# A third and a second seven-product group in the down stages of both FFNs

## The chip, the cores and the metric

The kernel runs on one core of one Trainium2 chip. The metric is the device time of one execution in microseconds (us), the median of several runs. The engines are TensorE (PE in the profile, with PEld for its weight loads), VectorE (DVE), ScalarE (ACT), GpSimd (POOL) and SyncE (SP), whose queue issues nearly all DMAs.

## What is computed

One encoder layer on 256 rows of width 2048, all in float32, with large feed-forward parts:

```python
def swiglu(h, w_gate, w_up, w_down):
    return (jax.nn.silu(h @ w_gate) * (h @ w_up)) @ w_down

x = x + 0.5 * swiglu(rms_norm(x, ffn1_norm), ffn1_w_gate, ffn1_w_up, ffn1_w_down)
...   # input projection, SSM, stick-breaking attention, output projection
x = x + 0.5 * swiglu(rms_norm(x, ffn2_norm), ffn2_w_gate, ffn2_w_up, ffn2_w_down)
...   # per-layer embedding
```

D_FF is 5632. The change is in the product with `w_down`: (256 x 5632) by (5632 x 2048), once in each FFN.

## The kernel before, in words

**Products in three parts.** Every float32 matrix is split into a high part (a cast to fp32r on ScalarE, L181) and a low part (the difference, on VectorE, L184). A product is then high x high, low x high and high x low, three matmuls of 128x512 each. Weights come from DRAM as tiles `raw` of 1 MB (512 rows by 512 columns, 128x2048 floats on chip); a split handles half of one (`whi`, `wlo`, 128x1024).

**The down stage** (from L649, in `ffn`) makes the four output blocks of 512 columns in two pairs, `n = 0` and `n = 2`. The inner dimension has 11 groups of 512 rows, `kb` 0 to 10. A plan (L673 to L676), one for each pair, says in which order the groups come and how each is computed:

- `cK` is a column step (`Seven.column`, L524): group K, first for one output block, then for the other. Each block takes two weight halves, and each half 12 matmuls (two row tiles of the output), so a column step has 48 matmuls, four weight splits and one split of the activations (`act`, L652: `hhi`, `hlo`).
- `sK` is a seven-product group (`Seven.chunk`, L490): group K for both blocks at once, by a Strassen-like scheme with 7 products instead of 8. Each product has 6 matmuls, 42 in all. It takes both weight tiles at once and forms four sums of weight halves on VectorE (`add`, L485 to L488, tile `sum`), which are split like weights (`shi`, `slo`); three other products split weight halves as they are (`whi`, `wlo`). It also takes sums of the activations, `sum_forms` (L432): four additions of 128x256 (L441, tile `rows`) and a split (`nhi`, `nlo`), beside the split of the activations themselves.
- `a5` is the rest, groups 5 to 10, first all of them for one block, then all for the other. There the activations are split again for the second block.

**Banks.** Products 2 and 4 (one block) and 3 and 8 (the other) end in the banks that the column steps use too. Products 1, 5, 6 and 7 have banks of their own; when the last `s` step of a pair has been issued, `opened` (L660 to L671) is put off to the next step: one copy on ScalarE (L663), and on VectorE two additions (L664, L669) and six of L658 that add these banks to the residual `x`. `end` (L686) adds the other banks to `x` and starts the norm of the next stage (`Normed.block`, L370): transposes on VectorE (L216), 32 small DMAs through SP's queue (L229), and later the split by L191 on ScalarE and L193 on VectorE, four of each for a block. For the two blocks of the first pair this falls into the second pair.

**What sets the order.** Each engine executes its instructions in the order of the program. A planner fixes that order when the kernel is built, from the order of the Python code, the readiness that it foresees and the free buffers: `raw` has five buffers, of which two hold `x` in the down stage; `whi` and `wlo` have four each, `shi` and `slo` three, `sum` two (shared by weight sums and `rows`), the activations of type `h` two.

Of the kernel before, what the change touches and what calls it, by code (L numbers as in the profile page):

```python
# [33 lines left out]
def layer_kernel(ctx: ExitStack, tc: tile.TileContext, a: dict, shapes: dict, out: bass.AP):  # L34
# [504 lines left out]
    def ffn(i, xn, nxt, bg=None):  # L539
# [120 lines left out]
        def opened(s, n):  # L660
# [10 lines left out]
            gather(xt[1][n + 1], one, -0.5)  # L671

        plans = (  # L673
            ("c2", "c3", "s0", "c4", "c5", "c6", "s1", "c7", "c8", "c9", "c10"),
            ("c1", "c2", "s0", "c3", "c4", "a5"),
        )  # L676
        for n in range(0, ND, 2):
            parts = {}
# [725 lines left out]

    n1, nm, n2, npl = Normed("ffn1_norm", load_turned), Normed("mix_norm"), Normed("ffn2_norm", kinds="hhnn", late=0), Normed("ple_norm", late=0)
    ffn(1, n1, nm, s5_prep)

    w_in = a["w_in"][0]
# [47 lines left out]
    mix.close()  # L1456

    ffn(2, n2, npl)


# [201 lines left out]
```

## Time and profile before

| what | value |
|---|---|
| median of 3 runs | 1852.45 us (1851.65 to 1853.28) |
| the profiled execution's own time | 1852.7 us |
| its span, first to last instruction | 1850.6 us |
| granted TensorE clock, mean | 1.000 |
| busy: PE, DVE, ACT, POOL | 1838.3, 1460.6, 1027.4, 63.3 us |
| matmuls | 9032 |
| read from DRAM, written | 373.46 MB, 11.93 MB |

The down stage of FFN 1 runs from 487.58 us to 724.40 us of the span, that of FFN 2 from 1506.75 us to 1742.38 us. In the views, a line of the timeline holds the start and the duration of an instruction, its engine, line, operation and operands; `x2` at its end says that two like it in a row were merged, and a bracket says how long the engine had been idle and who ended that. A matmul's duration in the profile (389 ns) is its way through the array; successive matmuls start closer together than that. The same holds for VectorE, where the next operation can start before the last has ended. The view by windows shows busy time of each engine in a stretch.

### The profile page before, as it was taken

Reading aid. Unit: us, or ns where it says so; the run is one execution under the profiler, and the core shown is the slowest. Engines: PE = TensorE matmul, PEld = TensorE weight load, DVE = VectorE, ACT = ScalarE, POOL = GpSimd, SP = SyncE. Lnnn points to the kernel's source line nnn. Section 1 sums busy time; section 2 is a strip of 40 time slices with the busy share of each in tenths; the row PEclk is TensorE's granted clock in tenths of the full one; section 3 lists DMA queues with packets and bytes.
Section 4 is the critical chain, followed back from the end, with each engine's and each line's share of the span. In section 5 each row is a group of like instructions: output and inputs, shape, how many; then the busy total and the mean of one; then the engine's idle time right before and its main releaser. Section 6 shows DMA issues by size and latency. Waiting matters only on the chain.

```text
span 1850.6 us, 23946 instructions
## 1 busy us (share of the span) xinstructions
PE 1838.3 (99%) x9032; PEld 1518.5 (82%) x9032; DVE 1460.6 (79%) x1718; ACT 1027.4 (56%) x1187; POOL 63.3 (3%) x108
## 2 busy tenths in 40 slices
PE   9999999999999999999999999999999999999998
PEld 7888888778888888888897888888888888888887
DVE  8967665998888876687567798989898978887665
ACT  7444443655564656365685565655555555565654
POOL 0011000000000000010021000000000000000000
PEclk9999999999999999999999999999999999999999
DMA  9888868566756567675646776665656675666663
GB/s 334 281 274 277 252 217 246 173 228 200 241 196 213 192 217 248 190 262 166 216 142 218 224 262 216 235 206 198 218 198 219 207 244 185 223 195 217 208 219 125
DMA packets 232307, 406.36 MB, mean 220 GB/s; under 512 B 26784, under 2 KB 50720, under 8 KB 231904
## 3 DMA queue, kind: packets, MB, share of 16 engines
q1 hardware_dynamic: 227824, 392.81, 63.8%
q0 software_dynamic: 3648, 10.62, 1.8%
q8 instruction: 70, 1.15, 0.2%
q10 hardware_dynamic: 720, 1.41, 0.2%
q14 instruction: 45, 0.37, 0.1%
HBM read 373.46 MB, written 11.93 MB: 208 GB/s over the span
## 4 chain that ended last, share of the span: by engine, by line
PE 92%; DVE 3%; DMA 2%; ACT 2%; SPq 1%; issue 1%; DVEq 0%; ACTq 0%
PE acc L305 18%; PE acc L310 18%; PE acc L306 18%; PE aux L305 7%; PE aux L306 7%; PE aux L310 7%; PE acc L480 3%; PE acc L481 2%; PE acc L483 2%; PE aux L480 2%; PE aux L483 2%; PE aux L481 2%; DVE wlo L184 1%; SPq L1170 1%; DMA raw<-in_w_in 1%
## 5 line engine op out<-in xcount | busy, mean ns | idle before, releaser
L181 ACT CAST whi<-raw 128x1024 fp32r<-128x1024 f32 x639 | 668.1, 1052 | 684.8 <-PE acc L306 388.9
L184 DVE TENSOR_TENSOR wlo<-raw,whi 128x1024 fp32r<-128x1024 f32 x639 | 772.0, 1221 | 297.9 <-ACT whi L181 295.1
L305 PE MATMUL acc<-whi,nhi 128*128 128x512 f32 x1232 | 482.9, 392 | 1.8 <-ACT whi L181 1.7
L306 PE MATMUL acc<-whi,nlo 128*128 128x512 f32 x1232 | 479.9, 390 | 0.0
L310 PE MATMUL acc<-wlo,nhi 128*128 128x512 f32 x1232 | 340.6, 389 | 0.2 <-DVE wlo L184 0.2
L305 PEld LDWEIGHTS acc<-whi,nhi 128*128 128x128 f32 x1232 | 231.5, 188 | 52.2 <-ACT whi L181 3.0
L310 PEld LDWEIGHTS acc<-wlo,nhi 128*128 128x128 f32 x1232 | 231.2, 188 | 48.8 <-DVE wlo L184 0.6
L306 PEld LDWEIGHTS acc<-whi,nlo 128*128 128x128 f32 x1232 | 231.6, 188 | 47.2
L306 PE MATMUL acc<-whi,hlo 128*128 128x512 f32 x376 | 146.4, 389 | 0.0
L305 PE MATMUL acc<-whi,hhi 128*128 128x512 f32 x376 | 146.3, 389 | 0.0
L181 ACT CAST shi<-sum 128x1024 fp32r<-128x1024 f32 x108 | 113.4, 1052 | 43.1 <-DVE sum L487 39.6
L306 PE MATMUL aux<-whi,hlo 128*128 128x512 f32 x344 | 133.8, 389 | 0.0
L305 PE MATMUL aux<-whi,hhi 128*128 128x512 f32 x344 | 133.8, 389 | 0.0
L184 DVE TENSOR_TENSOR slo<-sum,shi 128x1024 fp32r<-128x1024 f32 x108 | 130.9, 1216 | 0.6 <-ACT shi L181 0.5
L310 PE MATMUL acc<-wlo,hhi 128*128 128x512 f32 x376 | 114.6, 389 | 0.2 <-DVE wlo L184 0.2
L310 PE MATMUL aux<-wlo,hhi 128*128 128x512 f32 x344 | 106.0, 389 | 0.0
L306 PE MATMUL aux<-whi,nlo 128*128 128x512 f32 x240 | 93.4, 389 | 0.0
L305 PE MATMUL aux<-whi,nhi 128*128 128x512 f32 x240 | 93.4, 389 | 0.0
L306 PEld LDWEIGHTS acc<-whi,hlo 128*128 128x128 f32 x376 | 70.6, 188 | 15.1 <-DVE hlo L184 0.4
L310 PEld LDWEIGHTS acc<-wlo,hhi 128*128 128x128 f32 x376 | 70.5, 188 | 15.2 <-DVE wlo L184 0.6
L305 PEld LDWEIGHTS acc<-whi,hhi 128*128 128x128 f32 x376 | 70.6, 188 | 14.6
L306 PEld LDWEIGHTS aux<-whi,hlo 128*128 128x128 f32 x344 | 64.6, 188 | 13.5
(345 smaller groups left out, 2162.6 us busy)
## 6 DMA issues: line engine op xcount, KB each, us to landing
raw<-in_ffn_w_up SPq DMA_DIRECT2D x88, 1024.0 KB, 5.8
raw<-in_ffn_w_down SPq DMA_DIRECT2D x88, 1024.0 KB, 5.1
raw<-in_ffn_w_gate SPq DMA_DIRECT2D x86, 1024.0 KB, 6.2
raw<-in_w_in SPq DMA_DIRECT2D x32, 1024.0 KB, 5.7
raw<-in_w_out SPq DMA_DIRECT2D x16, 1024.0 KB, 5.3
raw<-in_w_ple_gate SPq DMA_DIRECT2D x16, 1024.0 KB, 5.1
hT<-mid SPq DMA_DIRECT2D x160, 64.0 KB, 3.5
h<-mid SPq DMA_DIRECT2D x176, 32.0 KB, 3.6
```

What stands on the lines that cost most here:

```text
L181: copy = nc.scalar.copy(hi, src)
L184: nc.vector.tensor_tensor(out=lo, in0=src, in1=hi.bitcast(F32), op=ALU.subtract)
L305: nc.tensor.matmul(ps[t], lhsT=lh, rhs=hi[:, j, cols], start=start and j == 0, stop=False)
L306: nc.tensor.matmul(ps[t], lhsT=ll, rhs=hi[:, j, cols], start=False, stop=False)
L310: nc.tensor.matmul(ps[t], lhsT=lh, rhs=lo[:, j, cols], start=False, stop=stop and j == 1)
L480: nc.tensor.matmul(ps, lhsT=lh[j], rhs=hi[:, j], start=begin and j == 0, stop=False)
L481: nc.tensor.matmul(ps, lhsT=ll[j], rhs=hi[:, j], start=False, stop=False)
L483: nc.tensor.matmul(ps, lhsT=lh[j], rhs=lo[:, j], start=False, stop=z in final and j == 1)
L1170: nc.sync.dma_start(zt[0][p1 : p1 + HC, z], sv[p0 : p0 + HC, r % 2 * 2 + r // 2])
```

## The change

Only the two plans differ. In the first pair a group moves from column steps to seven-product groups (three instead of two, and the groups are numbered anew); in the second pair too (two instead of one, with one column step between them). Both plans are used by both FFNs, so four of 44 steps of the two stages change their kind. The four sums in a group, the gate and up blocks and the DMAs of the weights are as before.

```diff
         plans = (
-            ("c2", "c3", "s0", "c4", "c5", "c6", "s1", "c7", "c8", "c9", "c10"),
-            ("c1", "c2", "s0", "c3", "c4", "a5"),
+            ("c3", "c4", "s0", "c5", "c6", "s1", "c7", "c8", "s2", "c9", "c10"),
+            ("c2", "c3", "s0", "c4", "s1", "a5"),
         )
```

## The prediction

> **What bounds the kernel now.** I read the first part of the page, then the chain that ended last, then windows of the down stages, and last the timelines of PE and VectorE there.
>
> ```profile
> span 1850.6 us, 23946 instructions
> PE 1838.3 (99%) x9032; PEld 1518.5 (82%) x9032; DVE 1460.6 (79%) x1718; ACT 1027.4 (56%) x1187; POOL 63.3 (3%) x108
> ...
> PEclk9999999999999999999999999999999999999999
> ...
> PE 92%; DVE 3%; DMA 2%; ACT 2%; SPq 1%; issue 1%; DVEq 0%; ACTq 0%
> ```
>
> TensorE is the bound: busy 99%, and 92% of the chain. So a matmul less is time less, as long as nothing else is late. VectorE at 79% is an average; the windows show what it hides. They are, in order: a seven-product group of FFN 1's first pair, two column steps behind it, the rest of that pair behind its last group (with `opened`) up to the second pair's group, the group of FFN 2's second pair, and the two column steps behind that one.
>
> ```profile
> core 0: us, PE busy (x) PEld busy (x) DVE busy (x) ACT busy (x) POOL busy (x), PEclk, DMA share, GB/s
> 509.34:518.98 9.64, 9.64 (x43) 7.89 (x42) 9.64 (x12) 6.34 (x7) 0.00 (x0) 1.00 0.64 221
> 529.86:551.62 21.76, 21.76 (x97) 18.02 (x96) 16.08 (x14) 12.34 (x13) 0.00 (x0) 1.00 0.45 165
> ...
> 561.30:626.50 65.20, 65.20 (x289) 54.03 (x288) 50.87 (x54) 36.98 (x45) 0.00 (x0) 1.00 0.56 190
> ...
> 1645.70:1655.35 9.65, 9.65 (x44) 7.89 (x43) 9.48 (x12) 8.13 (x12) 0.00 (x0) 1.00 0.95 325
> 1655.35:1677.11 21.76, 21.76 (x98) 18.02 (x97) 19.46 (x25) 10.42 (x11) 0.00 (x0) 1.00 0.65 232
> ```
>
> A column step takes PE 21.76/2 = 10.88 us (48 matmuls, 0.2267 us each), a group 9.64 us. In a group VectorE has next to no idle time (9.64 of 9.64, 9.48 of 9.65 us); in column steps it has. PE has none in any of these stretches.
>
> **What a swap saves.** 10.88 - 9.64 = 1.24 us of PE. There are four swaps: **-4.96 us**.
>
> **What a swap adds to VectorE.** The pace of VectorE is the distance of starts:
>
> ```profile
> 1640.21 1.22 DVE L487 TENSOR_TENSOR sum<-sum,raw 128x1024 f32<-128x1024 f32 x1
> ...
> 1650.43 1.21 DVE L184 TENSOR_TENSOR slo<-sum,shi 128x1024 fp32r<-128x1024 f32 x1
> 1651.81 2.36 DVE L184 TENSOR_TENSOR wlo<-raw,whi 128x1024 fp32r<-128x1024 f32 x2 [0.17 <-ACT whi L181]
> 1654.09 1.67 DVE L193 SCALAR_TENSOR_TENSOR nlo<-h,gains,nhi 128x256 fp32r<-128x256 f32 x4
> 1655.67 0.68 DVE L664 TENSOR_TENSOR sg<-aux,sg 128x512 f32<-128x512 f32 x1
> ...
> 1659.27 1.21 DVE L184 TENSOR_TENSOR wlo<-raw,whi 128x1024 fp32r<-128x1024 f32 x1
> ```
>
> ```profile
> 571.40 0.75 DVE L441 TENSOR_TENSOR rows<-hT 128x256 f32<-128x256 f32 x2
> ...
> 572.98 1.23 DVE L184 TENSOR_TENSOR wlo<-raw,whi 128x1024 fp32r<-128x1024 f32 x1
> ```
>
> The first two rows are ten operations of 128x1024 in a row: (1650.43 - 1640.21)/9 = 1.135 us each. Four of L193 take 1655.67 - 1654.09 = 1.58 us, six of `opened` 3.60 us (0.60 each), four of L441 1.58 us. A column step has five big operations, 5.7 us for 10.88 us of PE. A group has 13 (seven low parts, four sums, `hlo`, `nlo`) and the four small ones: 14.76 + 1.58 = 16.3 us for 9.64 us of PE. So every group takes 16.3 - 9.6 = 6.7 us of VectorE's lead over PE, and a column step gives back 10.9 - 5.7 = 5.2 us. The lead is bounded by the buffers: when it is full, VectorE waits for ScalarE, which waits for PE to free a weight buffer. Rows of FFN 1's first pair, behind the group that ended at 518.98:
>
> ```profile
> 514.21 1.21 DVE L184 TENSOR_TENSOR slo<-sum,shi 128x1024 fp32r<-128x1024 f32 x1
> ...
> 525.30 1.23 DVE L184 TENSOR_TENSOR wlo<-raw,whi 128x1024 fp32r<-128x1024 f32 x1 [0.36 <-ACT whi L181]
> 528.02 1.22 DVE L184 TENSOR_TENSOR wlo<-raw,whi 128x1024 fp32r<-128x1024 f32 x1 [1.49 <-ACT whi L181]
> ```
>
> ```profile
> 515.76 0.62 PE L483 MATMUL aux<-slo,nhi 128*128 128x512 f32 x2
> ```
>
> The last `slo` is ready at 515.42 and used at 515.76: a group that starts with a full lead ends with 0.34 us of it. Before 528.02, nine microseconds behind the group, the full wait of 1.49 us is back: with what was done ahead, one column step refills the lead.
>
> **First pair, both FFNs.** The new plan puts two column steps between groups and two behind the last. One refills the lead, so the third group starts like the second and costs PE nothing. `opened` moves behind it, with two column steps behind it now and four before, in which PE was busy throughout (65.20 of 65.20 us). Its 4.8 us fit into the slack of two steps, 2 x 5.2 us, and the first steps of the next pair follow. I take 0, with 0 and 1 us for each FFN as ends, since the lead shrinks to 0.34 us.
>
> **Second pair.** Here only `c4` stands between the groups, and it also carries the norm's two blocks (eight of L193). In the changed program, listed engine by engine, VectorE has this to do from the first `wlo` of `c4` to the first `wlo` of kb 6, in this order but for small swaps: 4 `wlo` of `c4` with the 8 of L193 between them; the group's 13 and 4 of L441; `hlo` and two `wlo` of kb 5, which the planner put ahead of the group's last `slo`; the 8 of `opened`; `hlo` and `wlo` of kb 6. That is 4 + 13 + 3 + 2 = 22 big operations, and the sum is 22 x 1.135 + 2 x 1.58 + 1.58 + 8 x 0.60 = 34.5 us. Nothing up to its start moves: it begins where the first group of the pair ends on VectorE, in FFN 1 when the weights of `c4` have landed,
>
> ```profile
> 632.83 2.00 ACT L181 CAST whi<-raw 128x1024 fp32r<-128x1024 f32 x2 [1.86 <-DMA raw<-in_ffn_w_down]
> ```
>
> ```profile
> 633.91 2.54 DVE L184 TENSOR_TENSOR wlo<-raw,whi 128x1024 fp32r<-128x1024 f32 x2 [0.70 <-ACT whi L181]
> 636.37 1.66 DVE L193 SCALAR_TENSOR_TENSOR nlo<-h,gains,nhi 128x256 fp32r<-128x256 f32 x4
> ```
>
> ```profile
> 636.57 0.39 PE L305 MATMUL acc<-whi,hhi 128*128 128x512 f32 x1
> ...
> 659.12 0.39 PE L305 MATMUL acc<-whi,hhi 128*128 128x512 f32 x1
> ```
>
> ```profile
> 1655.35 0.39 PE L305 MATMUL acc<-whi,hhi 128*128 128x512 f32 x1
> ```
>
> FFN 2: 1651.81 + 34.5 + 0.1 (the result is there 0.1 us after the next start) = 1686.4. FFN 1: the two `wlo` take 0.2 more, 633.91 + 34.8 = 668.7. PE begins that step at 1655.35 and 636.57. Without a stall it would need that `wlo` after 10.88 + 9.64 + 5.44 (kb 5 for one block) + 8 matmuls, 1.81 = 27.77 us: at 1683.1 and 664.3. So PE stalls **3.3 us in FFN 2 and 4.4 us in FFN 1**, however it is spread; the planner has put products 2 and 3 and matmuls of kb 5 between the late products, which moves PE's idle time back, not away. From there a half-step for one block costs VectorE 3.4 us for 5.44 us of PE, and the lead grows again. The stall at kb 6 costs a restart of 0.1 us in each FFN:
>
> ```profile
> 407.28 0.62 PE L483 MATMUL aux<-wlo,hhi 128*128 128x512 f32 x2
> 409.56 0.50 PE L480 MATMUL acc<-shi,nhi 128*128 128x512 f32 x1 [1.67 <-ACT shi L181]
> 409.90 0.39 PE L481 MATMUL acc<-shi,nlo 128*128 128x512 f32 x1
> ```
>
> (0.34 us between the first two starts behind a stall, not 0.23.) What goes: in FFN 1, `c3` and `c4` behind the old group took 659.12 - 636.57 = 22.55 us, 0.79 more than 21.76; that came from `opened` and the norm together in the first step, and `opened` is now elsewhere. **-0.79 us**.
>
> **ScalarE, SP, POOL.** ScalarE gets four casts more for a swap, 4 x 1.0 us by the row of two in 2.00; in a group it is busy 6.3 to 8.1 of 9.6 us, and I cost them at nothing (ends 0 and 1 us for a swap), since ScalarE idles in the column steps. One wait of its queue is new: `hhi` of kb 6 waits for PE to be done with the group's activations, product 4 last, and the `shi` of the group's fifth product stands behind it. VectorE has three operations, 3.4 us, between the `slo` of product 4 and the one that needs this `shi`; the way through two matmuls (0.45), their end (0.2) and two casts (2.0) takes 2.7: 0.7 us of margin. SP issues as many weight DMAs as before, in the same order around the norm's small ones; POOL's order is unchanged.
>
> **Sum.** -4.96 - 0.79 + 3.3 + 4.4 + 0.2 = **+2.2 us**. The profiled execution took 1852.7 us, 0.25 above the median; against the median 1852.45 + 2.2 = **1854.7 us**. Within 0.2% (3.7 us, about what a measurement can tell from no change: 1848.7 to 1856.2) I call it the same.
>
> **The pace against a rule.** The rows give 1.135 us from start to start, with durations of 1.22. The Trainium skill, "VectorE: DVE Perf Modes", section "The TRN2 errata", gives (N+151)/0.96 ns for an fp32 addition, 1224 ns at 1024, with latency exposed between instructions. Were that the pace, 22 operations would take 2.0 us more for each second pair, and the sum would be 1858.6; the trace agrees with the page on the duration and not on the pace, which decides.
>
> **Rivals.**
> 1. *Slower: the queues hold each other.* If that `shi` comes late, or the fifth product, for whose end L664 waits with all later `wlo` queued behind it, VectorE idles inside its list, and each microsecond is one of PE. Between the last `slo` and L664 stand two of L658, 1.2 us; PE needs 0.65 of it, and its own lateness the rest. For: the chain VectorE, PE, ScalarE, VectorE is closed here. Against: the margins are positive, 0.7 and up to 0.5. With 2 us in each FFN (two casts): 1858.7. It decides from 0.75 us in each FFN on. 0.27.
> 2. *Faster: no stall.* The interleaved matmuls would have to cover everything: 1852.45 - 5.75 = 1846.7. VectorE's list speaks against it; it would have to be 3 to 4 us shorter. 0.05.
> 3. *Half the stall*, if part of the norm's work moves ahead of the first group's end: 1850.8. 0.10.
> 4. *The clock falls.* The stall in one piece, 4.4 us in FFN 1, might lower the granted clock. In rows: 1.67 us of idle at 409.56, and the page shows PEclk at 9 in all 40 slices. If the matmuls behind it ran at double distance for 4.4 us: ten at +0.23, 1857.0. 0.05. The Trainium skill, "TensorE: Matmul & The Clock Gate", section "What's actually happening", has the clock halved after an idle window of about 3.4 us; no stall in this trace is that long.
> 5. *Operations of VectorE don't overlap*, and the list goes by durations of 1.22 (the rule above): 1858.6. Against: ten starts at 1.135. 0.03.
> 6. *It doesn't do what it says.* The words speak of weight sums by adding DMAs and of two groups in every gate and up block; the diff has neither. I forecast the diff: 24 matmuls less. If the words held, VectorE would lose two big operations in each group, and the stall with them. 0.
>
> **Chances.** The forecast 0.50 (1853 to 1856), and rival 3: within 0.2% 0.60. Slower: rivals 1, 4 and 5, 0.35. Faster 0.05. The range reaches from rival 3 to rival 1, 1850.8 to 1859.0: up to 4 us from the open ends above (ScalarE, the first pairs) lie in it. Left out are rival 2 and about half of rival 1, by which idle time could grow further.
>
> **What would show it.** 9008 matmuls. In both first pairs no idle PE behind the third group. In both second pairs PE idle behind `c4`, some 4 us, ended by VectorE (`slo`, `wlo`, `hlo`) and a little ScalarE, with VectorE busy without a gap for 34 us; a gap there is rival 1. PEclk 1.00. Wrong it would be if PE had no idle time at kb 6, or idle time in the first pairs.

## The result, and the profile after

The changed kernel takes **1854.68 us** (median, 1854.15 to 1855.66) against 1852.26 us (1851.49 to 1853.28) of the kernel before on the same chip: 2.4 us more, a ratio of 1.0014 with a 95% interval of 1.0007 to 1.002. The forecast was 1854.7 us. Its profiled execution took 1854.93 us, with a span of 1852.8 us, 2.2 us more than before.

The first part of the page of the kernel after:

```profile
span 1852.8 us, 23963 instructions
...
PE 1835.8 (99%) x9008; PEld 1512.9 (82%) x9008; DVE 1499.5 (81%) x1766; ACT 1041.7 (56%) x1203; POOL 62.6 (3%) x108
...
PEclk9999999999999999999999999999999999999999
```

24 matmuls are gone and PE is busy 2.5 us less, yet the span is longer: PE has new idle time. VectorE has 48 operations and 38.9 us more. Where PE waits, the windows of the same kernel tell (from the first pair of FFN 1 up to the first group of its second pair, then the second pair of each FFN from that group on; the first number behind the comma is PE's busy time):

```profile
core 0: us, PE busy (x) PEld busy (x) DVE busy (x) ACT busy (x) POOL busy (x), PEclk, DMA share, GB/s
500.00:625.49 125.49, 125.49 (x554) 103.61 (x552) 114.24 (x116) 77.59 (x86) 0.00 (x0) 1.00 0.59 196
625.49:636.40 10.91, 10.91 (x49) 8.96 (x48) 10.64 (x15) 8.84 (x12) 0.00 (x0) 1.00 0.95 322
...
646.10:657.00 10.90, 10.70 (x46) 8.02 (x45) 10.90 (x11) 6.99 (x9) 0.00 (x0) 1.00 0.29 99
657.00:668.00 11.00, 9.10 (x37) 6.62 (x37) 10.95 (x14) 6.28 (x7) 1.62 (x4) 1.00 0.50 188
...
1666.00:1676.00 10.00, 8.94 (x36) 6.25 (x36) 10.00 (x10) 6.09 (x8) 0.00 (x0) 1.00 0.31 105
1676.00:1687.00 11.00, 8.96 (x37) 6.28 (x36) 11.00 (x14) 6.98 (x8) 0.00 (x0) 1.00 0.53 192
```

In the first pair PE never stops, with three groups in it. In the second pairs it does, while VectorE is busy nearly all the time (10.90 of 10.90 and 10.95 of 11.00 us in FFN 1, all of it in FFN 2). PE's timeline there (the bracket is the idle time and who ended it):

```profile
663.94 0.50 PE L306 MATMUL acc<-whi,hlo 128*128 128x512 f32 x1 [1.22 <-DVE hlo L184]
...
666.28 0.97 PE L310 MATMUL acc<-wlo,hhi 128*128 128x512 f32 x3 [0.68 <-DVE wlo L184]
...
1684.25 0.50 PE L306 MATMUL acc<-whi,hlo 128*128 128x512 f32 x1 [1.22 <-DVE hlo L184]
...
1686.60 0.73 PE L310 MATMUL acc<-wlo,hhi 128*128 128x512 f32 x2 [0.68 <-DVE wlo L184]
```

These are the waits at kb 6, for `hlo` and for the `wlo` at the end of VectorE's list. A bracket counts from the modelled end of a matmul; the time lost is better taken from the starts. Wherever successive matmuls start over 0.30 us apart, I add up what is beyond 0.227 us: **3.32 us in FFN 1's second pair and 5.06 us in FFN 2's**, 8.38 us in all, in 9 and 14 gaps. The kernel before has 1.16 us there, all in FFN 1. Four swaps at -1.24 us and 8.38 - 1.16 us of idle time give -4.96 + 7.22 = +2.26 us, against +2.2 us of span and +2.4 us in the medians.

VectorE's list in the kernel after, its first operation, the end of the group and the last `wlo` (FFN 1, then FFN 2):

```profile
631.70 2.36 DVE L184 TENSOR_TENSOR wlo<-raw,whi 128x1024 fp32r<-128x1024 f32 x2 [0.27 <-ACT whi L181]
...
665.01 2.36 DVE L184 TENSOR_TENSOR wlo<-raw,whi 128x1024 fp32r<-128x1024 f32 x2
...
1648.88 1.22 DVE L184 TENSOR_TENSOR slo<-sum,shi 128x1024 fp32r<-128x1024 f32 x1
1652.07 2.36 DVE L184 TENSOR_TENSOR wlo<-raw,whi 128x1024 fp32r<-128x1024 f32 x2 [1.98 <-ACT whi L181]
1654.35 2.46 DVE L193 SCALAR_TENSOR_TENSOR nlo<-h,gains,nhi 128x256 fp32r<-128x256 f32 x6
...
1678.16 1.22 DVE L184 TENSOR_TENSOR slo<-sum,shi 128x1024 fp32r<-128x1024 f32 x1
...
1679.90 0.69 DVE L658 SCALAR_TENSOR_TENSOR x<-acc,x 128x512 f32<-128x512 f32 x1
1680.58 0.69 DVE L664 TENSOR_TENSOR sg<-aux,sg 128x512 f32<-128x512 f32 x1
...
1682.98 1.21 DVE L184 TENSOR_TENSOR hlo<-hT,hhi 128x1024 fp32r<-128x1024 f32 x1
1684.12 1.29 DVE L658 SCALAR_TENSOR_TENSOR x<-sg,x 128x512 f32<-128x512 f32 x2
1685.32 2.35 DVE L184 TENSOR_TENSOR wlo<-raw,whi 128x1024 fp32r<-128x1024 f32 x2
```

With 1.135 us for the last one, the list takes 665.01 - 631.70 + 1.135 = 34.4 us in FFN 1 and 1685.32 - 1652.07 + 1.135 = 34.4 us in FFN 2, where 34.5 was forecast. Only its start differs from the forecast, which took this start, and PE's steps beside it, from the kernel before. The first row of FFN 2 shows 1.98 us of idle time ahead of it (0.17 before), that of FFN 1 0.27 us (0.70 before). Behind this stand ScalarE's casts of the weights of `c4`, which waited for the DMA 1.43 us in FFN 1 (1.86 before) and 3.14 us in FFN 2 (1.32 before, the last row):

```profile
630.62 2.00 ACT L181 CAST whi<-raw 128x1024 fp32r<-128x1024 f32 x2 [1.43 <-DMA raw<-in_ffn_w_down]
...
1650.99 2.00 ACT L181 CAST whi<-raw 128x1024 fp32r<-128x1024 f32 x2 [3.14 <-DMA raw<-in_ffn_w_down]
```

```profile
1650.72 2.01 ACT L181 CAST whi<-raw 128x1024 fp32r<-128x1024 f32 x2 [1.32 <-DMA raw<-in_ffn_w_down]
```

### The profile page after: what moved, and what is told of

Same layout as the page of the kernel before. It is cut to its first block, busy times and chain, and to the rows that moved or that the text cites. A ratio compares the mean times of both kernels' runs of the same rounds, so it can differ in the third digit from the quotient of the medians.

```text
span 1852.8 us, 23963 instructions
## 1 busy us (share of the span) xinstructions
PE 1835.8 (99%) x9008; PEld 1512.9 (82%) x9008; DVE 1499.5 (81%) x1766; ACT 1041.7 (56%) x1203; POOL 62.6 (3%) x108
## 5 line engine op out<-in xcount | busy, mean ns | idle before, releaser
L305 PE MATMUL acc<-whi,nhi 128*128 128x512 f32 x1232 | 482.9, 392 | 1.7 <-ACT whi L181 1.6
L305 PEld LDWEIGHTS acc<-whi,nhi 128*128 128x128 f32 x1232 | 231.5, 188 | 52.1 <-ACT whi L181 2.6
L181 ACT CAST shi<-sum 128x1024 fp32r<-128x1024 f32 x124 | 130.2, 1051 | 46.3 <-DVE sum L487 42.9
L184 DVE TENSOR_TENSOR slo<-sum,shi 128x1024 fp32r<-128x1024 f32 x124 | 150.7, 1219 | 0.6 <-ACT shi L181 0.5
L306 PE MATMUL acc<-whi,hlo 128*128 128x512 f32 x344 | 133.8, 390 | 2.4 <-DVE hlo L184 2.4
L305 PE MATMUL acc<-whi,hhi 128*128 128x512 f32 x344 | 133.5, 389 | 0.0
L305 PE MATMUL aux<-whi,hhi 128*128 128x512 f32 x312 | 121.4, 389 | 0.0
L306 PE MATMUL aux<-whi,hlo 128*128 128x512 f32 x312 | 121.4, 389 | 0.0
L310 PE MATMUL acc<-wlo,hhi 128*128 128x512 f32 x344 | 104.8, 390 | 1.6 <-DVE wlo L184 1.4
L310 PE MATMUL aux<-wlo,hhi 128*128 128x512 f32 x312 | 96.1, 389 | 0.0
L305 PE MATMUL aux<-whi,nhi 128*128 128x512 f32 x240 | 93.4, 389 | 0.0
L310 PEld LDWEIGHTS acc<-wlo,hhi 128*128 128x128 f32 x344 | 64.2, 188 | 16.5 <-DVE wlo L184 3.3
L487 DVE TENSOR_TENSOR sum<-sum,raw 128x1024 f32<-128x1024 f32 x62 | 75.6, 1220 | 0.3
L305 PEld LDWEIGHTS acc<-whi,hhi 128*128 128x128 f32 x344 | 64.6, 188 | 13.4
```

The lines of the kernel that those rows point to most:

```text
L181: copy = nc.scalar.copy(hi, src)
L184: nc.vector.tensor_tensor(out=lo, in0=src, in1=hi.bitcast(F32), op=ALU.subtract)
L305: nc.tensor.matmul(ps[t], lhsT=lh, rhs=hi[:, j, cols], start=start and j == 0, stop=False)
L306: nc.tensor.matmul(ps[t], lhsT=ll, rhs=hi[:, j, cols], start=False, stop=False)
L310: nc.tensor.matmul(ps[t], lhsT=lh, rhs=lo[:, j, cols], start=False, stop=stop and j == 1)
L487: nc.vector.tensor_tensor(out=t, in0=x, in1=y, op=ALU.add)
```

## The experiments

**The theory**: the loss is the list of VectorE behind the one column step of the second pair. What shortens the list (the norm's work or `opened` moved out of it, a second column step between the groups) gives time back, and the first pair by itself is a gain. **The rival**: the queues hold each other, so that a part taken from the list is followed by another wait of the same size, and the time stays. Each edit is against the changed kernel if nothing else is said.

**1. The first pair alone.**

```diff
-            ("c2", "c3", "s0", "c4", "s1", "a5"),
+            ("c1", "c2", "s0", "c3", "c4", "a5"),
```

> Only the first pair's plan is the new one (three groups, two column steps between them); the second pair's is that of before. List theory (VectorE's queue behind a group, against PE's time for the column steps behind it): the lead is refilled in one column step, so PE idles nowhere in the first pairs and both swaps are a gain of 1.24 us: 1852.3 - 2.5 = 1849.8. Rival (a group costs elsewhere what it saves, wherever it stands): 1852.3, the same as before.

Measured: 1850.68 us, ratio 0.9993 (0.9984 to 1.0002). The interval reaches 1, so the times alone don't show the gain; the idle time of PE speaks for it: the first pairs have none. It is 0.9 us above the expected time, and the second pairs, whose plan is that of before, have 0.84 us of idle time in FFN 1 (1.16 before) and 1.16 us in FFN 2 (none before). A change in the first pair moves the start of the second.

**2. The second pair alone.**

```diff
-            ("c3", "c4", "s0", "c5", "c6", "s1", "c7", "c8", "s2", "c9", "c10"),
+            ("c2", "c3", "s0", "c4", "c5", "c6", "s1", "c7", "c8", "c9", "c10"),
```

> Only the second pair's plan is the new one; the first pair's is that of before. List theory: the loss is all here, 1854.7 + 2.5 = 1857.2, and PE idle of some 8 us in the two second pairs together, as in the changed kernel (8.4 us there). Rival (what the third group shifts in the first pair makes part of the loss): 1854 to 1855.5.

Measured: 1856.66 us, 1.0024 (1.0015 to 1.0032), with 3.18 and 4.54 us of idle PE. By the idle time the whole loss is in the second pair, and it is larger than that of the change as a whole.

**3. `opened` later.** In the second pair it is put off by 8 steps of the planner.

```diff
-                        put_off(0, opened, s, n)
+                        put_off(8 if n else 0, opened, s, n)
```

> The changed kernel with opened put off by 8 half-steps more in the second pair, to where the lead is full again. List theory: the 4.8 us of opened leave VectorE's list ahead of kb 6, and the two stalls at kb 6 (2.45 us each with restarts) go; what PE idles inside the group stays (0.9 us in FFN 1, 2.6 in FFN 2): 1854.7 - 4.9 = 1849.8. Rival (the stall at kb 6 is only what the planner's interleaving pushed back, and comes back elsewhere): 1854 to 1855.

Measured: 1850.09 us, 0.9986 (0.9977 to 0.9995). 4.8 us of VectorE's work moved, 4.6 us of time came back, and no gap is left at kb 6. What remains is 1.07 and 2.81 us ahead of it, in the group and in what is interleaved with it.

**4. The norm's split later.** The L191 and L193 work of the first two blocks starts 27 steps behind their transposes, not 11.

```diff
-                put_off(9 if soon else 11, self.parted, n, by_tile(out, 4))
+                put_off(27 if n < 2 and self.kinds == "nnnn" else 9 if soon else 11, self.parted, n, by_tile(out, 4))
```

> The changed kernel with the norm's split of the first two blocks (eight of L193 on VectorE, eight of L191 on ScalarE) put off by 16 half-steps more, out of the column step between the groups; opened stays where it was. List theory: VectorE's list ahead of the group and ahead of kb 6 is 3.2 us shorter in each FFN; the idle time of PE falls from 3.3 to about 0.5 us in FFN 1 and from 5.1 to about 1.9 us in FFN 2: 1854.7 - 6.0 = 1848.7. Rival (one column step between groups is too little whatever it carries, since ScalarE and the buffers bound it): 1853.5 to 1855.

Measured: 1850.18 us, 0.9987 (0.9978 to 0.9995): 4.5 us came back, less than the theory asked for and far from the rival. Idle PE is 1.17 and 2.36 us, where 0.5 and 1.9 were expected; what makes the difference is open.

**5. Both later** (the edits of 3 and 4 together).

> The changed kernel with both put off in the second pair, the norm's split by 16 and opened by 8 half-steps. List theory: the list ahead of kb 6 is 3.2 + 4.8 us shorter, more than PE idles there in either FFN (3.3 and 5.1 us), so what is left is what the weights of c4 come late (0 to 2 us in one FFN) and a few tenths: 1847.0, from 1846.3 to 1848.5. Rival (part of the stall belongs to one column step as such, with its buffers and ScalarE): 1848.8 or more, no better than one of the two alone by more than 1.5.

Measured: 1848.82 us, 0.9982 (0.9972 to 0.9991), a little over the expected range and just where the rival stands (1848.8 or more, and only 1.3 us below experiment 3). By the time alone, part of the stall could belong to the single column step as such; experiment 6, which keeps that step, decides. PE is idle 0.61 and 1.52 us, all of it in the group, and ScalarE still waits 1.60 and 2.50 us for the weights of `c4`. So the list was not all. A candidate is SP's queue: the norm's small DMAs stand ahead of those weights in SP's queue. SP in the kernel after, FFN 1 and FFN 2 (`x20` is twenty small DMAs; L295 is the first weight of `c4`):

```profile
611.67 13.24 SPq L229 DMA_DIRECT2D h<-mid  x20
625.01 0.53 SPq L295 DMA_DIRECT2D raw<-in_ffn_w_down  x1
...
1630.34 14.66 SPq L229 DMA_DIRECT2D h<-mid  x20
1645.10 0.53 SPq L295 DMA_DIRECT2D raw<-in_ffn_w_down  x1
```

The same place in the kernel before:

```profile
612.73 14.31 SPq L229 DMA_DIRECT2D h<-mid  x19
627.14 0.53 SPq L295 DMA_DIRECT2D raw<-in_ffn_w_down  x1
...
1631.89 13.13 SPq L229 DMA_DIRECT2D h<-mid  x19
1645.13 0.53 SPq L295 DMA_DIRECT2D raw<-in_ffn_w_down  x1
```

By the group's first matmul PE is 1.05 us earlier than before in FFN 1 and 1.55 us in FFN 2 (start at 625.49 and 1644.15, against 626.54 and 1645.70). The weight's DMA was issued 2.13 us earlier in FFN 1, but only 0.03 us in FFN 2: the block of small ones took 1.1 us less there and 1.5 us more here, with one DMA more in both. In FFN 1 of the kernel before, 1.8 us of the block was SP's queue waiting for the landing of a weight (`SPq L229 <- DMA raw<-in_ffn_w_down` in its waits), and in the changed kernel it has no such wait; in FFN 2 this wait is 0.5 us before and 0.6 after, and what is left of the 1.5 us is the one DMA more and some that took longer to issue.

**6. The small DMAs later too** (edit of 5, and the DMAs of L229 start 20 steps behind the transposes, not 6).

```diff
-                turn_quarters(out, mid, 4 if soon else 6)
+                turn_quarters(out, mid, 20 if n < 2 and self.kinds == "nnnn" else 4 if soon else 6)
```

> As the run with both put off, and the 32 small DMAs of the norm's two blocks are issued 14 half-steps later too, so that SP's queue holds none of them ahead of the weights of the second pair's group and of c4. If the late weights (VectorE idle 2.0 us ahead of c4 in FFN 2 of the changed kernel) come from these DMAs in SP's queue: no wait of ScalarE for raw ahead of c4, no idle PE in the second pairs, 1846.5 and 0 to 1.5 us below the run with both put off. If they come from the load of the DMA engines with weights alone: the wait stays, and the time is that of the other run.

Measured: 1846.84 us, 0.9971 (0.9961 to 0.998), 2.0 us below experiment 5, where at most 1.5 was expected. SP in this kernel, FFN 2; the first L295 row is the first weight of `c4`:

```profile
1627.17 3.15 SPq L229 DMA_DIRECT2D h<-mid  x5
1632.19 0.37 SPq L295 DMA_DIRECT2D raw<-in_ffn_w_down  x1
1632.61 9.19 SPq L229 DMA_DIRECT2D h<-mid  x12
```

The weight goes ahead of the block of twelve now (thirteen of the 32 still go ahead of it, 28 in the kernel after). The windows that lost two microseconds in the kernel after:

```profile
1666.00:1676.00 10.00, 10.00 (x45) 7.92 (x44) 9.77 (x9) 5.67 (x7) 0.00 (x0) 1.00 0.88 314
1676.00:1687.00 11.00, 11.00 (x50) 9.12 (x49) 11.00 (x16) 6.11 (x6) 0.00 (x0) 1.00 0.63 205
```

PE is busy 10.00 of 10.00 and 11.00 of 11.00 us; idle time is down to 0.39 and 0.12 us, and ScalarE has no wait for `raw` ahead of `c4`. All four swaps now pay, with a single column step between the groups as before, so the rival of experiment 5 falls. The small DMAs were not moved alone.

**7. Two column steps between the groups** of the second pair, nothing else.

```diff
-            ("c2", "c3", "s0", "c4", "s1", "a5"),
+            ("c2", "s0", "c3", "c4", "s1", "a5"),
```

> The changed kernel with another order in the second pair: c2, s0, c3, c4, s1, a5, two column steps between the groups and one ahead of the first; norm and opened are put off as in the changed kernel, which puts the norm's split into c3 and c4. List theory: the two column steps give 10.4 us, of which the norm takes 3.2 and the group before needs 6.7: the second group starts with nearly a full lead, and opened behind it costs 0 to 1 us in each FFN: 1847.5, from 1846.5 to 1849. Rival (a second group in the second pair does not pay, whatever stands between): 1852 or more.

Measured: 1848.37 us, 0.9979 (0.9969 to 0.9988), as the theory had it: 0.98 and 0.76 us of idle PE. One step more between the groups brings as much as moving the norm and `opened` (4.1 us below the kernel before, against 3.7). The first group also comes one step earlier in this order, which was not tried by itself.

**8. Three groups in the second pair**, on top of experiment 6.

```diff
-            ("c2", "c3", "s0", "c4", "s1", "a5"),
+            ("s0", "c3", "s1", "c4", "s2", "a5"),
```

> The run with all three put off, and the second pair with three groups and single column steps between them: s0, c3, s1, c4, s2, a5. By the list theory a column step without the norm gives back 5.2 of the 6.7 us that a group takes; the first group takes the full lead, so the second and the third find 1.5 and 3.0 us too little, of which the planner's interleaving with later column steps hides part: saving 2 x 1.24 = 2.5 more, stall 0 to 4.5 in each FFN: 1847.5, from 1844 to 1853. Rival (interleaving hides all of it as long as opened and the norm are away): 1844.

Measured: 1861.87 us (1857.64 to 1862.7), 1.0048 (1.0033 to 1.0063): a miss by 14 us. SP's queue in FFN 1, by its waits (total, times, longest) and then by time: it stands still 6.6 us for the norm's transposes (L216), which VectorE does at 600.79, issues fourteen small DMAs, and only then the second weight of `c3`, the one for its second output block (the first went out at 595.12):

```profile
SPq L229 <- DVE mid L216: 6.6, 1, 6.6
```

```profile
602.12 8.90 SPq L229 DMA_DIRECT2D h<-mid  x14
611.13 0.52 SPq L295 DMA_DIRECT2D raw<-in_ffn_w_down  x1
```

ScalarE waits for that weight:

```profile
617.76 1.99 ACT L181 CAST whi<-raw 128x1024 fp32r<-128x1024 f32 x2 [3.22 <-DMA raw<-in_ffn_w_down]
```

PE waits for ScalarE (L305 is a column step's, and `aux` the bank of its second block):

```profile
618.85 0.80 PE L305 MATMUL aux<-whi,hhi 128*128 128x512 f32 x1 [3.41 <-ACT whi L181]
```

And then the granted clock falls (windows; PEclk is the number ahead of the DMA share):

```profile
612.00:619.00 7.00, 3.26 (x14) 2.05 (x12) 6.24 (x7) 2.29 (x3) 0.00 (x0) 0.91 0.73 232
619.00:625.00 6.00, 6.00 (x15) 4.71 (x16) 5.33 (x7) 1.79 (x2) 0.00 (x0) 0.53 1.02 368
625.00:640.00 15.00, 15.00 (x67) 12.31 (x67) 11.79 (x12) 8.96 (x9) 0.00 (x0) 1.00 0.33 98
...
1641.00:1646.00 5.00, 4.44 (x12) 3.52 (x13) 5.00 (x7) 2.50 (x3) 0.00 (x0) 0.66 1.00 369
```

PE counts as busy in 6.00 of 6.00 us, yet it does 15 matmuls where at full clock 26 fit: they start 0.43 us apart, until 625. A busy share doesn't show this; PEclk and the count do. FFN 2 has the same at 1641, behind a gap of 2.66 us between two starts. Three runs had a mean clock of 0.996 or 0.997 and took 1861.7 us and more, the fourth 0.999 and 1857.64 us. How much of the wait is the queue's can only be argued. If the buffers of `raw` come round in turn, that weight takes the one of the group's first tile, which VectorE read last for the `wlo` of product 2:

```profile
607.71 1.23 DVE L184 TENSOR_TENSOR wlo<-raw,whi 128x1024 fp32r<-128x1024 f32 x1
```

That ends at 608.94, and the DMA was issued at 611.13. So the queue would have cost it 2.2 us of PE's 3.41, and the rest would be there without it. Another order of SP's queue was not tried here.

**9. Four groups in the first pair**, on top of experiment 6, with `opened` of the first pair put off by 4 steps.

```diff
-            ("c3", "c4", "s0", "c5", "c6", "s1", "c7", "c8", "s2", "c9", "c10"),
+            ("c4", "s0", "c5", "c6", "s1", "c7", "c8", "s2", "c9", "s3", "c10"),
...
-                        put_off(8 if n else 0, opened, s, n)
+                        put_off(8 if n else 4, opened, s, n)
```

> The run with all three put off, and a fourth group in the first pair: c4, s0, c5, c6, s1, c7, c8, s2, c9, s3, c10, opened of that pair put off by 4 half-steps. List theory: 2 x 1.24 us less of PE; the fourth group stands behind a single column step without the norm, which cost 0.5 and 0.1 us of idle PE in the second pairs of the other run, and opened meets the first steps of the next pair with a lead that is not yet full, 0 to 1 us for each FFN: 1845.2, from 1844.3 to 1847.5. Rival (a fourth group finds VectorE without lead, as the groups of the run with three in the second pair): 1849 or more.

Measured: **1846.14 us**, 0.9967 (0.9955 to 0.9978), the lowest median of all kernels here, 6.5 us below the kernel before. Against experiment 6 the two further swaps bring 0.7 us of the 2.5 that they save, a difference that the intervals of the two don't show. Idle PE is up from 0.51 to 1.55 us, and the rest is not located.

**10. One column step between two groups of the first pair**, second pair as in experiment 1.

```diff
-            ("c3", "c4", "s0", "c5", "c6", "s1", "c7", "c8", "s2", "c9", "c10"),
-            ("c2", "c3", "s0", "c4", "s1", "a5"),
+            ("c3", "c4", "s0", "c5", "s1", "c6", "c7", "c8", "s2", "c9", "c10"),
+            ("c1", "c2", "s0", "c3", "c4", "a5"),
```

> The first pair's plan alone, with one column step between its first two groups (c3, c4, s0, c5, s1, c6, c7, c8, s2, c9, c10); no norm work lies there, and opened stands behind the third group. The second pair as before. List theory: in program order the late products of the second group would wait 3 us for VectorE, but the column steps behind carry nothing else, so that interleaving hides most: 0 to 1 us of idle PE for each FFN, 1850.7 (the run with the first pair's new plan) + 0 to 2. Rival (a single column step costs as in the second pair, whatever it carries): 1850.7 + 7 = 1857.

Measured: 1851.17 us, 0.9994 (0.9984 to 1.0003), far from the rival's 1857 and not to be told from the kernel before by the times; and in each first pair one gap of 0.34 us, 0.11 us of idle time. So a single column step between groups costs next to nothing by itself. In the second pair the same step has the norm, `opened` and late weights beside it.

**The ledger.** Swaps against the kernel before (6 matmuls each) times -1.24 us, idle PE in the down stages less the 1.16 us of before, their sum, and the difference of the medians:

| kernel | swaps | idle PE, us | sum, us | measured, us |
|---|---|---|---|---|
| the change | 4 | 8.38 | +2.3 | +2.4 |
| 1 first pair | 2 | 1.99 | -1.6 | -1.7 |
| 2 second pair | 2 | 7.71 | +4.1 | +4.3 |
| 3 `opened` later | 4 | 3.88 | -2.2 | -2.3 |
| 4 norm later | 4 | 3.53 | -2.6 | -2.2 |
| 5 both later | 4 | 2.13 | -4.0 | -3.7 |
| 6 DMAs too | 4 | 0.51 | -5.6 | -5.6 |
| 7 two between | 4 | 1.73 | -4.4 | -4.1 |
| 8 three in the second pair | 6 | 17.36 | +8.8 | +9.4 |
| 9 four in the first pair | 6 | 1.55 | -7.0 | -6.5 |
| 10 one between | 2 | 2.69 | -0.9 | -1.4 |

In experiment 8, about 4 us of the idle column are gaps of 0.43 us under the lower clock. Every row closes within 0.7 us, so nothing of size lies elsewhere.

## Why the prediction was right

- **What a swap saves** (-1.24 us each): held. The ledger closes with it from two to six swaps.
- **First pair at 0**: held inside the first pairs, where no kernel with up to three groups has more than 0.12 us of idle PE. What it did not see is that the second pair is then reached in another state (experiment 1: 2.0 us of idle time there instead of 1.16).
- **VectorE's list, 34.5 us**: 34.4 us in both FFNs. The pace of 1.135 us held throughout, which settles rival 5. The Trainium skill, "VectorE: DVE Perf Modes", section "The TRN2 errata", agrees with the trace on the duration (1224 ns by its formula, 1.22 us in the rows) and not on the pace.
- **The stalls, 4.4 us in FFN 1 and 3.3 us in FFN 2, and 0.2 us for restarts**: this is the mis-sized term. Measured are 3.32 and 5.06 us, a sum of 8.4 instead of 7.9. The errors, -1.1 us in FFN 1 and +1.8 us in FFN 2, nearly cancel, and that is luck. The step that failed is "nothing up to its start moves". PE began `c4` in the kernel after at

```profile
635.13 0.39 PE L305 MATMUL acc<-whi,hhi 128*128 128x512 f32 x1
...
1653.79 0.39 PE L305 MATMUL acc<-whi,hhi 128*128 128x512 f32 x1
```

  so VectorE's lead at the start of the list was 635.13 - 631.70 = 3.43 us in FFN 1 (2.66 before) and 1653.79 - 1652.07 = 1.72 us in FFN 2 (3.54 before). By the prediction's own arithmetic PE needs the last `wlo` 27.77 us later, at 662.90 and 1681.56; it was there at 666.25 and 1686.56, 3.35 and 5.00 us late. The start moved against PE because PE came to the group 1.05 and 1.55 us earlier, while the weight's DMA, behind the small ones, came 2.13 us earlier in FFN 1 and 0.03 us in FFN 2. That the wait for `raw` is due to the place of the small DMAs in SP's queue, experiment 6 shows: it moved them, and the wait went.
- **What goes in FFN 1, -0.79 us**: it was 1.16 us. Inside the old group one more gap stood, between these two starts of the kernel before (0.54 us, and 0.34 behind it):

```profile
632.72 0.40 PE L481 MATMUL aux<-shi,nlo 128*128 128x512 f32 x1
633.26 0.74 PE L483 MATMUL aux<-slo,nhi 128*128 128x512 f32 x2
```

  This 0.4 us and the 0.5 us above cancel nearly, which is luck too, and why the total came out closer than its terms.
- **SP's queue**: "the same order" was nearly true (28 small DMAs ahead of the first weight of `c4` in both kernels, but 20 instead of 19 in the last block) and not enough. In FFN 2 the block took 1.5 us more, and VectorE's lead at the start of the list fell by 1.8 us.
- **Rival 1**, the queues hold each other: it did not occur. L664 started 1680.58 - 1679.90 - 0.60 = 0.08 us late in FFN 2 and 0.14 us late in FFN 1 (660.27 behind an L658 at 659.53), and no other row of VectorE's list has a gap, so that `shi` was not waited for either. Experiments 3, 4 and 7 gave back 4.5 to 6.3 us, where the rival expected nearly nothing.
- **Rivals 2 and 3** (no stall, half of it) fell by the 8.4 us. Experiment 6 is what rival 2 described, 1846.8 us, and needs the moved work for it.
- **Rival 4**, the clock: 1.00 in all windows of the kernel after; the stall came in pieces (the largest gap between starts is 1.61 us). Experiment 8 shows that the mechanism is real.
- **Rival 6**: 9008 matmuls, as the diff has it.

## What to carry to other kernels

Price a step on the bound engine, then list what the engine that feeds it must do between two of its deadlines, from start to start, with everything that happens to fall there: here two small jobs of 3.2 and 4.8 us and a block of small DMAs, not the groups themselves, made a gain of 5.6 us into a loss of 2.4. Deferrable work belongs behind the stretch in which the lead is thin. And check when that list can start: a queue of small DMAs ahead of one large load moves it.

## What the hardware showed

- A block of 19 or 20 small DMAs (32 KB each) holds up SP's queue for 13.1 to 14.7 us, 0.66 to 0.75 us each with the waits among them, and a 1 MB load behind them waits that long. Where five go between two weights (experiment 6) they take 3.15 us, 0.63 us each.
- In experiment 8 the granted clock fell at a gap in PE's work of 3.41 us in FFN 1 and 2.26 us in FFN 2 (3.80 and 2.66 us between two starts), each with two gaps of 0.7 us between starts in the seven before. PE's matmuls then started 0.43 us apart, for some 6 us in FFN 1 and some 3 us in FFN 2, and then 0.227 again. The windows place the fall:

```profile
614.40:617.70 3.30, 0.73 (x2) 0.30 (x2) 3.30 (x4) 0.13 (x1) 0.00 (x0) 1.00 0.73 227
617.80:618.80 1.00, 0.00 (x0) 0.00 (x0) 0.27 (x1) 1.00 (x2) 0.00 (x0) 0.50 0.77 279
...
1638.40:1641.70 3.30, 0.87 (x3) 0.44 (x4) 3.30 (x4) 1.24 (x2) 0.00 (x0) 1.00 0.82 245
1641.80:1645.10 3.30, 3.30 (x9) 2.53 (x9) 3.30 (x4) 0.96 (x2) 0.00 (x0) 0.50 1.05 405
```

  In FFN 1 that is 617.70 to 617.80, some 2.3 us after PE's last work ended (618.85 - 3.41 = 615.44) and before the gap was over; in FFN 2 it is 1641.70 to 1641.80, when PE had just come back. The Trainium skill, "TensorE: Matmul & The Clock Gate", section "What's actually happening", has the clock halved after an idle window of about 3.4 us and the window running freely. In neither case had PE been idle for 3.4 us when the clock fell, so 3.4 us is no safe bound here. Gaps of 1.6 us between starts left PEclk at 1.00.
